# A two-layer decoder trunk on one core: expert products in two passes by branches, whole-unit weight splits, and operands at even places

## The chip, the core and the metric

One NeuronCore of a Trainium2 chip runs the whole program. The metric is device time in microseconds (us), the median of several executions; lower is better. The engines named below are TensorE (PE; its weight loads are PEld), VectorE (DVE), ScalarE (ACT), GpSimd (POOL) and the queue engine that issues transfers (SP). A letter q behind an engine's name (PEq, DVEq) is its sequencer.

## The reference

256 tokens of width 1024 pass through two layers. Each layer has an attention mixer and a channel mixer; the channel mixer of layer 0 is a dense SwiGLU of width 3584, and that of layer 1 sends each token to its best two of eight experts. All of it is float32.

```python
def moe_swiglu(h, router_w, w_gate, w_up, w_down):
    t = h.reshape(B * S, D)                                  # 256 x 1024
    logits = (t @ router_w).astype(jnp.float32)
    top_v, top_i = lax.top_k(logits, TOP_K)                  # 2 of 8
    top_w = jax.nn.softmax(top_v, axis=-1)
    gates = jnp.sum(jax.nn.one_hot(top_i, N_EXPERTS) * top_w[..., None], axis=1)
    y = jnp.zeros_like(t)
    for e in range(N_EXPERTS):                               # each 3 x 1024 x 3584 weights
        y = y + gates[:, e:e + 1] * ((jax.nn.silu(t @ w_gate[e]) * (t @ w_up[e])) @ w_down[e])
    return y
```

With the inputs that the reference draws by default, the eight experts get 68, 62, 71, 84, 60, 28, 77 and 62 tokens (counted by running the reference's own routing). Experts 1, 4, 5 and 7 have at most 64.

## The kernel before

**Precision.** Every weight is split in two float32r parts: ACT copies a piece into the high part (L139, the tile w), DVE subtracts that from the original to get the low part (L159, the tile lo). Activations are split likewise. A product is three matmuls into one PSUM bank: high by high, high by low, low by high.

**The stream of weights.** The class Stream brings the weights in units of 128 partitions x 2048 columns (1 MB) into a ring of raw buffers (L120, issued by SP when the buffer's last reader, usually DVE's subtraction, is done), and splits them in pieces of 1024 columns, in a fixed order that a planner has written out. There are four places for high parts and four for low ones; in layer 1 the attention mixer's accumulator row becomes a fifth high place (widen), and the mixer's q, k and v buffers and one more become raw buffers (extend), so that the expert stage has 12 raw buffers. get() hands the next piece to PE; pump() and rest() issue the splits for pieces to come as far as the places allow.

**The expert stage** (experts, 8 experts x 7 chunks of 512 columns). For each pair of experts, pick() builds one-hot matrices from the token's place in its expert (posm), gather() multiplies them with the tokens' high and low parts (L972), and ACT copies the up to 128 tokens of an expert, as columns, into xe (L974). A chunk then runs in this order: gate (wide, L986, 24 matmuls of 128 x 512), SiLU on ACT (L1107), up (wide, L986, 24 matmuls), and down of the chunk before (L1029, 24 matmuls into ps_y). Within the next gate's matmuls, turn() transposes the activation (L1012, four transposes) and splits it (L400 on ACT, L401 on DVE). The product of SiLU and up (L1125) is made by DVE in two halves among the down matmuls. After the last chunk of an expert, finish() puts the gated rows back in place with matmuls by the transposed one-hots (back, L1055, L1056), among the matmuls of the next expert. In the very last chunk down comes after its own transposes.

**The overflow.** An expert with more than 128 tokens is completed in a branch (overflow, L1159) that all engines read and skip here: each loads the largest count into a register (L1158) and branches over a loop that has hundreds of matmuls.

**Places.** A tile's place is worked out from the order and the sizes of the tiles in the pools. Before, the raw buffers begin at byte 28,640 of a partition, which is 895 x 32, an odd multiple of 32 bytes, and so do the splits, xe and the activation's parts (g_hi, g_lo); the dense layer's and the mixers' activations (dg_hi, onT_hi, hT_hi) lie at even multiples.

## Time and profile before

| what | value |
|---|---|
| median of 3 runs | 1525.04 us (1522.99 to 1525.07) |
| the profiled execution | 1523.73 us, of which 1521.6 us are its span |
| mean granted TensorE clock | 0.995 of full speed |
| busy share of the span | PE 98%, DVE 85%, ACT 69%, POOL 1% |
| moved by transfers | 481.81 MB, mean 317 GB/s |

The span runs from the first to the last instruction; 2.1 us of the execution lie outside it. A busy PE is not a PE at its peak, since matmuls are pipelined and their shown durations overlap: the time from the start of one matmul to the start of the next is what counts.

### The profile page before, as it was taken

What the parts mean: (1) busy time and instruction counts of PE and PEld (TensorE: products, weight loads), DVE (VectorE), ACT (ScalarE), POOL (GpSimd) and SP (SyncE); (2) the same over time, 40 slices, a digit from 0 to 9 for tenths busy, and PEclk for the clock granted to TensorE, in tenths of its full rate; (3) what the DMA queues carried; (4) which work ended last, traced back from release to release, by engine and by line L of the source; (5) the groups of instructions that cost most, each with busy time, mean ns of one, the idle gap of its engine ahead of it and who ended that gap; (6) DMA issues with size and microseconds to landing.
All of it is one profiled execution on the core that took longest, in us unless ns stands there. A gap on an engine that the chain in (4) does not pass through costs nothing.

```text
span 1521.6 us, 21909 instructions
## 1 busy us (share of the span) xinstructions
PE 1492.3 (98%) x7985; PEld 1271.4 (84%) x7985; DVE 1288.5 (85%) x1601; ACT 1054.0 (69%) x1404; POOL 20.2 (1%) x20
## 2 busy tenths in 40 slices
PE   8999999999999899999999999999999999999998
PEld 7988999999898688888888888888888888888886
DVE  5988877777876678899889889889889888988987
ACT  5575644444666578777787777777777778777775
POOL 1000000000020000000000000000000000000000
PEclk9999999999999999999999999999999999999999
DMA  9974778778572379999989999989999998999980
GB/s 368 415 271 166 295 269 324 292 278 314 192 264 111 123 294 368 380 368 360 367 332 353 376 375 358 370 331 350 374 377 363 362 364 334 358 374 372 352 344 28
DMA packets 68481, 481.81 MB, mean 317 GB/s; under 512 B 7953, under 2 KB 8593, under 8 KB 10770
## 3 DMA queue, kind: packets, MB, share of 16 engines
q1 hardware_dynamic: 68178, 480.33, 83.0%
q8 instruction: 63, 1.03, 0.3%
q14 instruction: 48, 0.39, 0.1%
q0 software_dynamic: 192, 0.05, 0.0%
HBM read 479.25 MB, written 1.05 MB: 316 GB/s over the span
## 4 chain that ended last, share of the span: by engine, by line
PE 63%; DVE 1%; issue 0%; ACT 0%; DVEq 0%
PE ps_y L1029 20%; PE ps_gate L986 20%; PE ps_up L986 20%; PE ps_gt L1012 2%; PE ps_g L972 1%; PE ps_sc L1055 0%; PE ps_sc L1056 0%; DVE lo L159 0%; DVE pick L877 0%; PE ps_sc L1079 0%; ACT g_hi L400 0%; PE ps_b L882 0%; DVE fin L1087 0%; ACT junk L355 0%; DVE x_sb L1081 0%
## 5 line engine op out<-in xcount | busy, mean ns | idle before, releaser
L159 DVE TENSOR_TENSOR lo<-raw,w 128x1024 fp32r<-128x1024 f32 x810 | 949.3, 1219 | 43.5 <-ACT w L139 39.8
L139 ACT ACTIVATE w<-raw 128x1024 fp32r<-128x1024 f32 x810 | 832.1, 1059 | 187.6 <-PE ps_gu L350 73.6
L986 PE MATMUL ps_gate<-w,xe 128*128 128x512 f32 x896 | 302.9, 398 | 0.0
L986 PE MATMUL ps_up<-w,xe 128*128 128x512 f32 x896 | 289.8, 392 | 0.0
L986 PEld LDWEIGHTS ps_up<-w,xe 128*128 128x128 f32 x896 | 168.3, 188 | 36.2
L986 PEld LDWEIGHTS ps_gate<-w,xe 128*128 128x128 f32 x896 | 168.4, 188 | 34.3
L986 PE MATMUL ps_up<-lo,xe 128*128 128x512 f32 x448 | 175.4, 392 | 0.3
L986 PE MATMUL ps_gate<-lo,xe 128*128 128x512 f32 x448 | 175.1, 391 | 0.1
L1029 PE MATMUL ps_y<-w,g_hi 128*128 128x512 f32 x440 | 137.7, 392 | 0.0
L1029 PE MATMUL ps_y<-lo,g_hi 128*128 128x512 f32 x440 | 137.3, 391 | 0.0
L1029 PE MATMUL ps_y<-w,g_lo 128*128 128x512 f32 x440 | 137.2, 391 | 0.0
L349 PE MATMUL ps_gu<-dT_hi,w 128*128 128x256 f32 x432 | 121.2, 281 | 0.0
L350 PE MATMUL ps_gu<-dT_lo,w 128*128 128x256 f32 x432 | 120.8, 280 | 0.0
L351 PE MATMUL ps_gu<-dT_hi,lo 128*128 128x256 f32 x432 | 120.7, 279 | 0.0
L400 ACT ACTIVATE g_hi<-ps_gt 128x512 fp32r<-128x512 f32 x55 | 32.9, 598 | 105.4 <-PE ps_gt L1012 105.4
L401 DVE TENSOR_TENSOR g_lo<-ps_gt,g_hi 128x512 fp32r<-128x512 f32 x55 | 38.1, 692 | 78.6 <-ACT g_hi L400 77.8
L986 PEld LDWEIGHTS ps_up<-lo,xe 128*128 128x128 f32 x448 | 84.2, 188 | 19.8 <-DVE lo L159 2.0
L986 PEld LDWEIGHTS ps_gate<-lo,xe 128*128 128x128 f32 x448 | 84.4, 188 | 16.5 <-DVE lo L159 0.8
L1029 PEld LDWEIGHTS ps_y<-lo,g_hi 128*128 128x128 f32 x440 | 82.7, 188 | 17.9
L1029 PEld LDWEIGHTS ps_y<-w,g_lo 128*128 128x128 f32 x440 | 82.7, 188 | 17.6
L1029 PEld LDWEIGHTS ps_y<-w,g_hi 128*128 128x128 f32 x440 | 82.4, 188 | 17.3
L349 PEld LDWEIGHTS ps_gu<-dT_hi,w 128*128 128x128 f32 x432 | 81.3, 188 | 1.4 <-issue 0.2
(295 smaller groups left out, 1935.9 us busy)
## 6 DMA issues: line engine op xcount, KB each, us to landing
raw<-in_w_moe_dram SPq DMA_DIRECT2D x336, 1024.0 KB, 6.6
raw<-in_w_early_dram SPq DMA_DIRECT2D x114, 1024.0 KB, 7.0
raw<-in_w_early_dram SPq DMA_DIRECT2D x6, 512.0 KB, 9.3
gate<-in_ada_b_dram SPq DMA_DIRECT2D x4, 512.0 KB, 5.6
x_sb<-in_x_dram SPq DMA_DIRECT2D x1, 1024.0 KB, 7.5
out_dram<-fin SPq DMA_DIRECT2D x4, 256.0 KB, 2.1
fg<-in_final_g_dram SPq DMA_DIRECT2D x1, 512.0 KB, 3.3
cn<-in_consts_dram SPq DMA_DIRECT2D x1, 192.0 KB, 13.4
```

Of the source, the lines that this page charges most:

```text
L139: self.nc.scalar.activation(hi, raw, AF.Copy)
L159: self.nc.vector.tensor_sub(parts[1], raw, parts[0].bitcast(F32))
L349: nc.tensor.matmul(out_, lh, rh, start=start, stop=False)
L350: nc.tensor.matmul(out_, lh, rl, start=False, stop=False)
L351: nc.tensor.matmul(out_, ll, rh, start=False, stop=stop)
L400: nc.scalar.activation(hi, src, AF.Copy)
L401: nc.vector.tensor_sub(lo, src, hi.bitcast(F32))
L972: nc.tensor.matmul(ps[:, i], part[:, b, k * P:(k + 1) * P], pk[:, b], start=(b == 0), stop=(b == NB - 1))
L986: nc.tensor.matmul(ps, lh, w[:, c], start=(k == 0 and lh is xe_hi and w is hi), stop=(k == KD - 1 and lh is xe_lo))
L1012: nc.tensor.transpose(ps[:, i], act[:, (f0 + i) * P:(f0 + i + 1) * P], ident)
L1029: nc.tensor.matmul(y_ps[e][hf], lh, w[:, hf * 512:(hf + 1) * 512], start=(ch == 0 and f == 0 and lh is g_hi and w is hi), stop=(last and l ...
```

## The change

1. **Two passes.** If an expert has at most 64 tokens (NARROW), its tokens are gathered to every second column (slotm = posm x 2). The columns 0, 2, 4, ... of the 256 that hold its high and its low part side by side are then one stationary operand: 64 high columns and 64 low ones. Two matmuls, by the high and by the low part of the weight, give all four products, the low rows in partitions 64 to 127. folded() adds these to the upper rows: ACT copies them to SBUF, one matmul of 64 rows (onto) adds them in PSUM. In turn() the narrow transposes write each row to two columns (eight transposes in place of four). In down the rows are left apart; the transposed one-hot of the pair (now made by POOL, pickb) adds both when the rows are put back.
2. **Branches.** The counts of all experts are loaded into PE registers, and every group of products (twelve or eight matmuls), the transposes and the folds stand in a branch on the expert's count, on PE alone: by_width() twelve times a chunk for products, once for the transposes; add() twice.
3. **Whole units.** In the expert stage a unit is split by one instruction of 2048 columns on each of ACT and DVE. There are two such high and low places in the split tiles, and the mixer's q and k buffers are two more high ones, v one more low one; they are no raw buffers any more, and the further raw buffer is gone: 8 raw buffers remain.
4. **Places.** The tiles are reordered and gaps are put between pools, so that raw buffers, splits, xe and the activations' parts all begin at multiples of 512 bytes.
5. The product of SiLU and up is one DVE instruction of 512 columns, behind the fold; SiLU moves behind the gate's fold, into the up matmuls.

```diff
+    def whole(self, high, low):
+        self.size = RAW
+        ...
     def prep(self, lazy=False):
-        u, o, what = self.pieces[self.next_prep]
+        u, o, n, what = self.pieces[self.next_prep]
         self.load()
-        raw = self.raw[u][:, o:o + SPLIT]
+        raw = self.raw[u][:, o:o + n]
...
+    def half(self):
+        if not self.rest_of:
+            hi, lo = self.get()
+            self.rest_of = [(hi[:, c:c + SPLIT], lo[:, c:c + SPLIT]) for c in range(0, hi.shape[-1], SPLIT)]
+        return self.rest_of.pop(0)
...
+    gap(keep, 384)
+    cn = keep.tile([P, C_MASK], F32, name="cn")
...
+    gap(keep, 160)
+    gap(tiny, 96)
...
+        if l:
+            whi = [qkv_pool.tile([P, RAW], F32R, tag=tag, name="whi2") for tag in "qk"]
+            ws.whole(whi, [qkv_pool.tile([P, RAW], F32R, tag="v", name="wlo2")])
...
+        nc.gpsimd.tensor_scalar(less, iota, NARROW - 0.5, -float(NARROW), ALU.is_gt, ALU.mult)
+        nc.gpsimd.tensor_sub(base, iota, less)
+        nc.gpsimd.tensor_scalar(onto[:, NARROW:], ident[:, NARROW:], 0.0, None, ALU.mult)
+        nc.gpsimd.tensor_copy(onto[:, :NARROW], ident[:, NARROW:])
...
+        def by_width(e, wide, narrow):
+            with tc.If(held[e] > NARROW) as cmp:
+                wide()
+            with cmp.Else():
+                narrow()
...
             for j in range(2):
+                slot = outer.tile([P, CAP], F32, name="slot", bufs=2)
+                nc.gpsimd.tensor_scalar(slot, less, stretch[:, e + j:e + j + 1], None, ALU.mult)
+                nc.gpsimd.tensor_add(slot, slot, base)
+                pb = outer.tile([P, NB, CAP], F32, name="pickb", bufs=2)
+                for b in range(NB):
+                    nc.gpsimd.tensor_scalar(pb[:, b], slot, posm[:, b, e + j:e + j + 1], None, ALU.is_equal)
+                rows_of.append(pb)
...
+            nc.vector.tensor_scalar(stretch, ps_p[:, 2], NARROW + 0.5, 1.0, ALU.is_lt, ALU.add)
+            nc.vector.tensor_tensor(slotm, posm, stretch[:, None, :].to_broadcast([P, NB, E]), ALU.mult)
...
+            nc.vector.tensor_copy(count, ps_p[:, 2])
+            held.extend(nc.tensor.value_load(count[0:1, e:e + 1], min_val=0, max_val=S) for e in range(E))
             overflow(l, hT, posm, gating, gates, most, [put.args[-1] for put in puts])
...
             def wide(e, ps):
                 for k in range(KD):
-                    xe_hi, xe_lo = xe[e][k]
-                    c = halves[k % 2]
                     if k % 2 == 0:
-                        hi, lo = ws.get()
-                    for lh, w in ((xe_hi, hi), (xe_hi, lo), (xe_lo, hi)):
-                        nc.tensor.matmul(ps, lh, w[:, c], start=(k == 0 and lh is xe_hi and w is hi),
-                                         stop=(k == KD - 1 and lh is xe_lo))
+                        hi, lo = ws.half()
+                        def products(*passes):
+                            n = 0
+                            for kk in range(k, k + 2):
+                                both = xe[e][kk]
+                                for part, w in passes:
+                                    n += 1
+                                    nc.tensor.matmul(ps, both[:, part], w[:, halves[kk % 2]], start=(k == 0 and n == 1),
+                                                     stop=(k == KD - 2 and n == 2 * len(passes)))
+                        first, second, even = slice(0, CAP), slice(CAP, 2 * CAP), slice(0, 2 * CAP, 2)
+                        by_width(e, partial(products, (first, hi), (first, lo), (second, hi)),
+                                 partial(products, (even, hi), (even, lo)))
                     yield k
+            def folded(ps):
+                t = pool.tile([P, FC], F32R, name="fold", bufs=2)
+                nc.scalar.activation(t[NARROW:], ps[NARROW:], AF.Copy)
+                by = partial(nc.tensor.matmul, ps, onto[NARROW:], t[NARROW:], start=False, stop=True, ...)
+                def add(e):
+                    with tc.If(held[e] <= NARROW):
+                        by()
+                return add
...
-                        nc.tensor.transpose(ps[:, i], act[:, (f0 + i) * P:(f0 + i + 1) * P], ident)
-                    split(hi[:, :n], lo[:, :n], ps)
+                    by_width(e, partial(turns, slice(0, P), slice(0, P)),
+                             partial(turns, slice(0, NARROW), slice(0, P, 2), slice(1, P, 2)))
+                    split(both[:, :n, 0], both[:, :n, 1], ps)
...
+                    add = folded(pg)
                     act = pool.tile([P, FC], F32, name="act")
-                    nc.scalar.activation(act, pg, AF.Silu)
...
                     for k in wide(e, pu):
+                        if k == 3:
+                            add(e)
+                            nc.scalar.activation(act, pg, AF.Silu)
```

## Rows read from the trace of the kernel before

**Rows 1.** The profile page, its part 1 (busy time, share of the span, instructions of each engine) and, of its part 2 (the span in 40 equal slices), the busy tenths of the DMA engines and the GB/s.

```profile
PE 1492.3 (98%) x7985; PEld 1271.4 (84%) x7985; DVE 1288.5 (85%) x1601; ACT 1054.0 (69%) x1404; POOL 20.2 (1%) x20
...
DMA  9974778778572379999989999989999998999980
GB/s 368 415 271 166 295 269 324 292 278 314 192 264 111 123 294 368 380 368 360 367 332 353 376 375 358 370 331 350 374 377 363 362 364 334 358 374 372 352 344 28
```

**Rows 2.** The view of stretches, one row for each (from:to in us, its length, then busy us and instructions of PE, PEld, DVE, ACT and POOL, the granted clock, the mean busy share of the DMA engines, GB/s): the start with layer 0's mixer, the dense layer, layer 1's mixer with the routing, the expert stage.

```profile
0.00:160.00 160.00, 147.84 (x996) 132.01 (x997) 127.32 (x247) 97.84 (x219) 10.25 (x14) 0.99 0.76 300
160.00:392.00 232.00, 232.00 (x1645) 215.56 (x1644) 179.35 (x225) 107.85 (x142) 0.00 (x0) 1.00 0.80 295
392.00:534.00 142.00, 132.94 (x903) 118.64 (x901) 99.17 (x207) 88.00 (x200) 9.92 (x6) 0.98 0.48 171
534.00:1492.00 958.00, 957.38 (x4360) 789.32 (x4360) 860.66 (x897) 744.06 (x819) 0.00 (x0) 1.00 0.93 355
```

**Rows 3.** The chain of work that ended last, in order of time (start us, us, what), over one chunk of an expert, into the next.

```profile
702.20 4.10 PE ps_gate L986 x18
706.29 0.44 PE ps_gt L1012 x4
706.73 1.38 PE ps_gate L986 x6
708.11 5.48 PE ps_up L986 x24
713.59 5.49 PE ps_y L1029 x24
719.08 4.12 PE ps_gate L986 x18
```

**Rows 4.** The same view of stretches as in Rows 2: one of the start, in which many loads are under way at once, and the steady part of the expert stage.

```profile
10.00:70.00 60.00, 57.23 (x455) 55.95 (x455) 47.53 (x76) 33.70 (x62) 1.68 (x3) 0.97 1.02 418
540.00:1480.00 940.00, 939.55 (x4272) 774.58 (x4271) 849.09 (x887) 731.81 (x804) 0.00 (x0) 1.00 0.94 360
600.00:640.00 40.00, 40.00 (x183) 32.95 (x182) 34.22 (x36) 30.06 (x34) 0.00 (x0) 1.00 0.97 372
```

**Rows 5.** DVE and ACT in order of time (start us, us from the first start to the last end, engine, line, what, how many; in brackets the idle time before).

```profile
708.01 8.03 DVE L159 TENSOR_TENSOR lo<-raw,w 128x1024 fp32r<-128x1024 f32 x7
...
708.68 6.00 ACT L139 ACTIVATE w<-raw 128x1024 fp32r<-128x1024 f32 x6
```

**Rows 6.** Groups of instructions by line and shape (line, engine, operation, out<-in, shapes, count | busy us, mean ns of one | idle us before, and what ended it): the DVE and ACT work of the expert stage.

```profile
L159 DVE TENSOR_TENSOR lo<-raw,w 128x1024 fp32r<-128x1024 f32 x810 | 949.3, 1219 | 43.5 <-ACT w L139 39.8 <-PE ps_w L350 2.6 <-ACTq L1159 0.5
L139 ACT ACTIVATE w<-raw 128x1024 fp32r<-128x1024 f32 x810 | 832.1, 1059 | 187.6 <-PE ps_gu L350 73.6 <-PE ps_y L1029 41.7 <-PE ps_gate L986 17.0
...
L401 DVE TENSOR_TENSOR g_lo<-ps_gt,g_hi 128x512 fp32r<-128x512 f32 x55 | 38.1, 692 | 78.6 <-ACT g_hi L400 77.8
...
L400 ACT ACTIVATE g_hi<-ps_gt 128x512 fp32r<-128x512 f32 x55 | 32.9, 598 | 105.4 <-PE ps_gt L1012 105.4
...
L1058 DVE SCALAR_TENSOR_TENSOR x_sb<-ps_sc,gates,x_sb 128x512 f32<-128x512 f32 x28 | 20.9, 746 | 0.0
...
L1050 DVE TENSOR_TENSOR y_lo<-yt,y_hi 128x512 fp32r<-128x512 f32 x14 | 9.6, 685 | 0.0
...
L1042 DVE TENSOR_TENSOR yt<-ps_y,gate 128x512 f32<-128x512 f32 x14 | 9.6, 683 | 0.0
```

**Rows 7.** The same view: PE's matmuls of 512 columns, those of the expert stage (both operands at odd places) and those of the dense layer (stationary at an even place, moving at an odd one), the transposes, and a weight load.

```profile
L986 PE MATMUL ps_up<-lo,xe 128*128 128x512 f32 x448 | 175.4, 392 | 0.3
...
L1029 PE MATMUL ps_y<-lo,g_hi 128*128 128x512 f32 x440 | 137.3, 391 | 0.0
...
L986 PEld LDWEIGHTS ps_gate<-lo,xe 128*128 128x128 f32 x448 | 84.4, 188 | 16.5 <-DVE lo L159 0.8
...
L349 PE MATMUL ps_d<-w,dg_hi 128*128 128x512 f32 x112 | 44.4, 397 | 0.0
L350 PE MATMUL ps_d<-lo,dg_hi 128*128 128x512 f32 x112 | 44.4, 396 | 0.0
```

**Rows 8.** The overflow's branch, line L1159: the sequencers' instructions there (count: duration ns min/median/max, first and last start us).

```profile
L1159 ACTq COMPARE_BRANCH  x1: 50/50/50, 526.1 to 526.1; - x1
L1159 POOLq COMPARE_BRANCH  x1: 45/45/45, 526.1 to 526.1; - x1
L1159 PEldq COMPARE_BRANCH  x1: 3446/3446/3446, 526.2 to 526.2; - x1
...
L1159 DVEq COMPARE_BRANCH  x1: 72/72/72, 526.5 to 526.5; - x1
L1159 DVEq EVENT_SEMAPHORE  x1: 21/21/21, 527.1 to 527.1; - x1
...
L1159 PEldq EVENT_SEMAPHORE  x1: 51/51/51, 529.7 to 529.7; - x1
```

**Rows 9.** PE and its weight loads in order of time, where the first expert's gate begins behind a short idle time (columns as in Rows 5).

```profile
534.75 0.19 PEld L986 LDWEIGHTS ps_gate<-w,xe 128*128 128x128 f32 x1
534.78 0.48 PE L986 MATMUL ps_gate<-w,xe 128*128 128x512 f32 x1
...
535.10 0.40 PE L986 MATMUL ps_gate<-lo,xe 128*128 128x512 f32 x1
```

**Rows 10.** The load of the overflow's count into PE's register (columns as in Rows 8), and PE behind the branch (columns as in Rows 5).

```profile
L1158 PEldq TENSOR_LOAD <-most x1: 492/492/492, 525.6 to 525.6; - x1
...
529.93 0.77 PE L972 MATMUL ps_g<-pick,h_hi 128*128 128x256 f32 x2 [4.60 <-PEq L1159]
...
533.72 0.69 PE L882 MATMUL ps_b<-cn,pick 128*128 128x128 f32 x2
```

**Rows 11.** Groups of POOL's instructions (columns as in Rows 6).

```profile
L862 POOL CAST ident<-cn 128x128 bf16<-128x128 f32 x1 | 1.2, 1156 | 10.4 <-issue 10.4
...
L862 POOL CAST ones<-cn 128x128 bf16<-128x128 f32 x1 | 0.3, 288 | 0.0
```

More of the change, by code (lines that the diff above doesn't have):

```diff
@@ L43 @@
 CAP = P
+NARROW = 64
 V_ADAB, V_ATTN, V_FFN, V_QN, V_KVN, V_OUT, V_FB = 0, 48, 56, 64, 66, 67, 75
@@ L105, in extend, with widen @@
             self.load()
-    def widen(self, pool, tag):
-        self.turns.insert(0, (pool, tag, 1))
+    def widen(self, tile_):
+        self.turns.insert(0, Place(tile_))
+    def whole(self, high, low):
+        self.size = RAW
+        turns = []
+        for t, old, more in zip(self.split, (self.turns, self.low_turns), (high, low)):
+            new = [Place(x) for x in more]
+            for at in range(0, SPLIT_BUFS * SPLIT, RAW):
+                new.append(Place(t, at))
+                new[-1].last = max(x.last for x in old if x.tile is t and at <= x.at < at + RAW)
+            turns.append(new)
+        self.turns, self.low_turns = turns
     def load(self, most=None):
@@ L169, in pump @@
         while self.next_prep < len(self.pieces) and (most is None or n < most):
-            if self.pieces[self.next_prep][2] is None:
+            _, _, size, what = self.pieces[self.next_prep]
+            if what is None:
+                if size > self.size:
+                    break
                 ahead = len(self.turns) - (self.prepped >= self.given + need)
-                if self.prepped >= self.released + ahead:
+                if self.prepped >= self.released + ahead or self.turns[0].last >= self.released:
                     break
@@ L194, in get @@
     def get(self, n=1):
+        assert not self.rest_of
         self.settle()
@@ L341, in trunk_kernel @@
     for y in order:
-        pieces.append((*place[y], y[1:] if y[0] == "ada" else None))
+        u, o = place[y]
+        if y[0] not in "gud":
+            pieces.append((u, o, SPLIT, y[1:] if y[0] == "ada" else None))
+        elif not o:
+            pieces.append((u, o, sources[u][1], None))
     ws = Stream(nc, sources, pieces, raw_pool, split_pool, fold)
@@ L1021, in down, with products @@
                 for f in range(NFC):
-                    hi, lo = ws.get()
-                    g_hi, g_lo = g[f]
-                    last = ch == CH - 1 and f == NFC - 1
-                    steps = [(hf, lh, w) for lh, w in ((g_hi, hi), (g_hi, lo), (g_lo, hi)) for hf in range(2)]
-                    if last:
-                        steps.sort(key=lambda s: s[0])
-                    for hf, lh, w in steps:
-                        nc.tensor.matmul(y_ps[e][hf], lh, w[:, hf * 512:(hf + 1) * 512],
-                                         start=(ch == 0 and f == 0 and lh is g_hi and w is hi),
-                                         stop=(last and lh is g_lo))
+                    hi, lo = ws.half()
+                    both = g[f]
+                    def products(*passes):
+                        first, last = ch == 0 and f == 0, ch == CH - 1 and f == NFC - 1
+                        steps = [(n, hf) for n in range(len(passes)) for hf in range(2)]
+                        if last:
+                            steps.sort(key=lambda s: s[1])
+                        for n, hf in steps:
+                            part, w = passes[n]
+                            nc.tensor.matmul(y_ps[e][hf], both[:, part], w[:, halves[hf]], start=(first and n == 0),
+                                             stop=(last and n == len(passes) - 1))
+                    first, second, even = slice(0, CAP), slice(CAP, 2 * CAP), slice(0, 2 * CAP, 2)
+                    by_width(e, partial(products, (first, hi), (first, lo), (second, hi)),
+                             partial(products, (even, hi), (even, lo)))
                     yield f
@@ L1119, in experts @@
                             step()
-                    parts = deque(slice(c, c + FC // 2) for c in (0, FC // 2))
+                    parts = deque([slice(0, FC)])
+                    add = folded(pu)
                     def product():
                         if parts:
+                            add(e)
                             c = parts.popleft()
```

108 lines of the change are left out of this document (61 added, 47 removed).

## The prediction

> **What bounds the kernel now.** I read the page first. PE is busy for 98% of the span, but DVE is at 85% and the DMA engines are at nine tenths from the middle of the span on [rows 1], so the share alone does not say what a faster PE would give. The view of stretches divides it: the expert stage is 958 of 1521.6 us, with PE busy throughout, DVE for 90% and the DMA engines for 93% of it [rows 2]. The chain that ended last decides: over whole chunks it is PE alone, matmul behind matmul, without a wait for a split or a load [rows 3]. One chunk, from the first gate matmul to the next chunk's, lasts 719.08 - 702.20 = 16.88 us, and its parts are gate 4.10 + 1.38, transposes 0.44, up 5.48, down 5.49 [rows 3]. 24 matmuls in 5.48 us are 0.228 us each, start to start. So PE is the bound, and 56 chunks of 16.88 us are 945 us. The reader is to see the second thing too: DVE and the loads are close behind it, and they are what a chunk with less PE work runs into.
>
> **What the change removes from PE.** Four experts have at most 64 tokens, so 28 of 56 chunks are narrow. Each loses 24 of 72 matmuls and gains two folds and four transposes: 48 x 0.228 = 10.9, folds 0.46, transposes 2 x 0.44 = 0.88, in all 12.3 us. A stationary operand that takes every second column could load more slowly; the load takes 188 ns [rows 7] and a matmul 228, and even if each pair then took 0.30 us, PE would stand at 15.8 us, no worse than what follows.
>
> **What holds a narrow chunk then.** Three things, each from its own row.
>
> Loads. A chunk is six units of 1.049 MB. In the start, with many loads under way, the DMA engines gave 418 GB/s at a full share [rows 4]: 2.51 us a unit, 15.05 us a chunk. Over the expert stage they gave 360 GB/s at a share of 0.94 [rows 4]; if that was already their way of working there, full means 383 GB/s and 16.4 us. I lean to the first, since the second is measured with gaps between the loads, and keep both.
>
> DVE. Seven subtractions of 1024 columns take 8.03 us [rows 5], so one follows another by (8.03 - 1.22) / 6 = 1.135 us. From 692 ns at 512 columns to 1219 at 1024 [rows 6] a column costs 1.03 ns; 2048 columns take 1.135 + 1.054 = 2.19 us, six of them 13.1. The product and the low part of the activation are one 512-column instruction each, 0.69 less the same overlap of 0.08 us: 1.2 together. Putting back an expert's rows is 2 x 0.683 + 2 x 0.685 + 4 x 0.746 = 5.7 us [rows 6], with overlap 5.1, or 0.7 a chunk. Sum 15.1 us. With pieces of 1024 it would be 12 x 1.135 + 2.0 = 15.6, so whole units give DVE half a microsecond a chunk, worth nothing where PE is the bound.
>
> ACT. Six copies in 6.00 us [rows 5] follow each other by 0.99 us; the slope from 598 ns to 1059 is 0.90 ns a column [rows 6], so a unit takes 1.91 and six take 11.5 us. SiLU, the high part and the two new fold copies are 4 x 0.5 = 2.0. ACT also stands still before each high part, 105.4 us over 55 times, for the transposes [rows 6]: 1.9 us. That is 15.4 us, and the fold copies add two more places where ACT waits for PE, with four high places to have run ahead.
>
> Three floors of 15.05 to 15.4 us do not mesh perfectly: I take 15.8 us for a narrow chunk, a gain of 1.08 us, times 28 = **-30 us**. The ends: 15.05 us gives -51, 16.4 gives -13.
>
> **Wide chunks.** They keep 72 matmuls, and the other engines stay under 16.88 us, so they keep their time unless the places change the matmul. With both operands at odd places a matmul shows 391 to 392 ns, with the stationary one at an even and the moving one at an odd place 396 to 397 [rows 7]: a step of 5 ns when the two differ. The dense layer's down, the value projection and the output projections, 624 matmuls that differ now, would lose it: **-3 us**. No row shows two even operands of this kind at 512 columns often enough. If being even is worth the same step again, 72 x 28 x 0.005 = 10 us come off; if it costs it, 10 us come on; I take nothing. The Trainium skill (TensorE: Matmul & The Clock Gate, Back-to-back issue gap) gives N / 2.4 + 2.5 ns, 216 ns at 512 columns; the 228 ns here lie above it, and if the new places brought that figure, an estimate from the page, wide chunks would lose 24 us more and the sum would be 1470.
>
> **The start of the stage.** PE loads eight counts into registers ahead of the overflow's branch, where PE is the last to come out [rows 8, 10]. One load takes 0.49 us [rows 10]; together they cost between 0.49, if they overlap, and 3.9 us: I take **+3 us**, since the next step waits for all of them. POOL makes the first pair's pickb, eight instructions of 128 x 128, while PE is in the branch and the gather. POOL's casts of that shape take 0.29 and 1.16 us [rows 11]; PE's transposes come at 533.72 [rows 10], 8 us behind the counts, so 2.3 to 9.2 us of work cost 0 to 1.4 us, and I take 0. Later pairs' one-hots can be made many chunks ahead.
>
> **The branches.** There are 15 a chunk. A sequencer's compare and branch took 45 to 72 ns on ACT, POOL and DVE, and 3,446 ns on PE, which skipped the longest code [rows 8]. The arms here skip a few instructions, so I take the short price. It is hidden by the matmuls that are queued ahead: 12 matmuls last 2.7 us. I cost it at nothing; without that cover it would be 15 x 0.07 = 1 us a chunk.
>
> **Sum** against the profiled execution: 1523.7 - 30 - 3 + 3 = 1493.7, or **1494 us**; the median of the runs is 1.3 us above that execution, so the gain is 31 us or 2.0%. Its own range, from the ends of the narrow chunk and the places: 1470 to 1512.
>
> **Rival 1, slower: PE empties at branches.** Counts that other engines wait for must agree on both arms. The skipped overflow shows how the program settles this: a semaphore instruction on PE's sequencer (51 ns) behind the branch [rows 8]. If the shorter arm ends in such an instruction, and it waits for the matmuls before it, PE runs dry. The price: the rest of the last matmul 0.39 - 0.23 = 0.16, the instruction 0.05, the way from it to the next matmul 0.1 to 0.2 (529.7 to 529.93 with another wait between [rows 8, 10]), and a first matmul of 0.48 in place of 0.39 [rows 9]: about 0.45 us. The shorter arm is the narrow one for the twelve groups of products, the wide one for transposes and folds. A narrow chunk is then 12.3 + 12 x 0.45 = 17.7 us (+0.8), a wide one 16.88 + 1.35: 28 x 0.8 + 28 x 1.35 = +60 us, **1585 us**. It decides from a price of about 0.3 us, where a narrow chunk reaches 15.9 and the wide ones lose 25 us. For it: the instruction is there in the trace. Against it: it is seen once, on an idle PE, and a last matmul could carry the count itself. If both arms waited everywhere, 15 times 0.45, the time would pass 1750.
>
> **Rival 2, slower: a branch that has to fetch code.** PE's one branch took 3.45 us [rows 8]. If one branch in every chunk did, a narrow chunk would hide it (12.3 + 3.4 = 15.7) and a wide one not: 28 x 3.4 = 97 us, less the gain, **1590 us**. For it: twelve more groups of matmuls in each chunk are code that is skipped. Against it: the other engines' branches were short. The Trainium skill (Runtime: NRT & Kernel Launch, Instruction fetch mechanics) says that a taken branch to a target outside the fetched window stalls for a fetch; the 3.45 us agree with that, and short skips mostly stay inside it.
>
> **Rival 3: the loads are the bound already.** At 383 GB/s a narrow chunk takes 16.4 us and the gain is 13 us: **1511 us**. For it: a share of 0.97 at 372 GB/s in a full stretch [rows 4]. Against it: 418 GB/s in the start. Four fewer raw buffers would push the same way.
>
> **How the numbers follow.** The forecast has 0.44; a gain beyond its range, by the places, 0.08; rival 3 has 0.12, rival 1 0.25, rival 2 0.05, and 0.06 remain for a gain and a branch cost that cancel. What this kernel's runs can tell from no change is about 0.2%. Faster: 0.44 + 0.08 + 0.12 = 0.64; slower 0.30; same 0.06. The range must reach into rival 1, which alone has more than two in ten: 1465 to 1600 us leaves out some 0.05 below and 0.13 above.
>
> **What would show it.** Right: in narrow chunks PE has gaps that end in a split or a load, the chunk lasts 15.5 to 16.2 us, the DMA share is full and the rate above 400 GB/s; wide chunks stay at 16.9 us; 512-column matmuls show 385 to 392 ns everywhere. Rival 1: semaphore rows on PE's sequencer by the hundred, and in the chain "issue" or PEq pieces between groups of eight matmuls. Rival 2: a few dozen compare-and-branch rows of over 3 us. Rival 3: a full share at under 390 GB/s. The prediction is wrong if a branch costs PE more than 0.3 us, if ACT's waits at the folds hold up the splits, or if other counts of tokens arrive.

## The result, and the profile after

The changed kernel takes 1534.33 us (1533.29 to 1536.63, four runs) beside 1524.45 us for the kernel before on the same chip: a ratio of 1.0066, with a 95% interval of 1.0054 to 1.0079. It is slower by 0.7%, where 1494 us were forecast. The profiled execution has a span of 1531.5 us, 9.9 us above the 1521.6 before.

From the page after: PE's busy time, and by slices of 38 us the DMA engines' share in tenths and what they moved.

```profile
PE 1436.7 (94%) x7481; PEld 1159.0 (76%) x7481; DVE 1272.4 (83%) x1212; ACT 1073.7 (70%) x1180; POOL 51.4 (3%) x56
DMA  9974778778571249999999899998999998999992
GB/s 374 403 269 165 289 273 314 288 280 307 191 273 58 82 171 349 358 351 358 418 368 342 339 348 339 349 354 317 368 426 396 381 414 346 339 352 353 361 416 117
```

PE shows 504 matmuls fewer than before [rows 1], and the rate now goes up and down in the expert stage: its slices above 400 GB/s belong to narrow experts. The view of stretches (columns as in [rows 2]), for the whole stage and for two stretches of narrow chunks:

```profile
534.00:1496.00 962.00, 900.50 (x3870) 675.04 (x3871) 840.86 (x513) 761.44 (x601) 32.17 (x29) 0.99 0.92 356
720.00:760.00 40.00, 37.19 (x156) 25.78 (x155) 38.99 (x26) 34.91 (x26) 0.00 (x0) 1.00 1.00 418
1120.00:1160.00 40.00, 37.11 (x149) 25.83 (x150) 38.76 (x22) 36.53 (x28) 0.00 (x0) 1.00 1.01 419
```

And PE's time line where two chunks begin, first a wide one (expert 2) and its successor, then a narrow one (expert 4) and its successor; each row is the first gate matmul.

```profile
861.20 0.39 PE L1071 MATMUL ps_gate<-whi,xe 128*128 128x512 f32 x1
879.21 0.39 PE L1071 MATMUL ps_gate<-whi,xe 128*128 128x512 f32 x1
...
1111.91 0.39 PE L1071 MATMUL ps_gate<-whi,xe 128*128 128x512 f32 x1
1127.05 0.39 PE L1071 MATMUL ps_gate<-whi,xe 128*128 128x512 f32 x1
```

The narrow chunk takes 15.14 us. Six units at 418 GB/s take 15.05, and the DMA engines are at a full share; but DVE is busy for 97% of these stretches too. The view of waits over the expert stage (560 to 1500 us; who waited for whom, us in all, times, longest) decides between them:

```profile
PE ps_gate L1071 <- DVE wlo L183: 20.6, 30, 1.0
```

It has no line in which an engine waits for a load. By the order of loads and splits, each unit of the undisturbed narrow chunks landed at least 5 us before ACT began to split it. So a narrow chunk is bound by DVE's splits, and the loads just keep up.

The wide chunk takes 18.01 us, where it took 16.88 [rows 3]. With the first gate of every chunk read in this way, the whole difference can be laid out. (An expert's stretch runs from its first gate matmul to the next expert's, so it begins with the last down of the expert before.)

| stretch | before | after | difference |
|---|---|---|---|
| up to the first gate matmul | 534.8 | 549.5 | +14.7 |
| the four wide experts (0, 2, 3, 6) | 479.6 | 513.2 | +33.6 |
| the four narrow experts (1, 4, 5, 7) | 472.7 | 433.4 | -39.3 |
| from the last gate on | 34.5 | 35.5 | +1.0 |
| sum | 1521.6 | 1531.5 | +9.9 |

(The parts are rounded, the sums are the spans.) So the narrow experts gained more than forecast, and two terms that were put at 0 and +3 took it all back: the wide chunks and the way to the first gate.

**Wide chunks.** The views of the two lines of branches: instructions, nanoseconds (least, median, most), first and last start. L1088 is the fold's branch in add(), L933 that of by_width().

```profile
L1088 PEldq COMPARE_BRANCH  x168: 67/176/358, 556.1 to 1509.3; - x168
L1088 PEldq EVENT_SEMAPHORE  x56: 51/51/51, 559.9 to 1398.3; - x56
...
L933 PEldq COMPARE_BRANCH  x1093: 65/176/428, 549.3 to 1518.6; - x183
```

There are 56 semaphore instructions, two for each of 28 wide chunks, all at the fold, which has no arm for wide experts. The branches at L933, whose two arms both hold matmuls, have none. The time line around one of them:

```profile
869.38 0.39 PE L1071 MATMUL ps_up<-wlo,xe 128*128 128x512 f32 x1
869.61 0.39 PE L1071 MATMUL ps_up<-whi,xe 128*128 128x512 f32 x1
870.12 0.60 ACT L1231 ACTIVATE act<-ps_gate 128x512 f32<-128x512 f32 x1 [0.28 <-PEq L1088]
870.31 0.49 PE L1071 MATMUL ps_up<-whi,xe 128*128 128x512 f32 x1 [0.32 <-PEq L1088]
870.64 0.39 PE L1071 MATMUL ps_up<-wlo,xe 128*128 128x512 f32 x1
```

From 869.38 to 869.61 is the usual 0.23 us. The next matmul comes 0.70 us later, when the one before has ended and the sequencer has passed the semaphore, and the one after that 0.33 us later: 0.57 us lost, twice a chunk. Each of the 56 semaphore instructions starts 0.04 us behind the end of the last matmul ahead of it, so PE has run empty by then. The reader should see that PE was idle for the sequencer, and that ACT's SiLU waits for the same instruction: it stands for the fold's matmul in the count that SiLU waits for.

**The way to the first gate.** The eight loads of counts (their three instructions), the overflow's branch on PE, and PE's first matmuls behind it:

```profile
L1037 PEldq TENSOR_LOAD <-count x8: 299/302/494, 531.7 to 536.9; - x8
L1037 PEldq FUSED_REGOPS  x8: 146/146/160, 532.3 to 537.3; - x8
L1037 PEldq SEQ_ASSERT  x8: 18/18/24, 532.5 to 537.5; - x8
...
L1279 PEldq COMPARE_BRANCH  x1: 6187/6187/6187, 538.0 to 538.0; - x1
...
544.48 0.77 PE L1052 MATMUL ps_g<-pick,h_hi 128*128 128x256 f32 x2 [14.59 <-PEq L1279]
```

The loads stand one behind another from 531.72 to 537.58, 0.73 us each, and the branch that took 3.45 us [rows 8] takes 6.19. PE is idle for 14.59 us, where it was for 4.60 [rows 10]. The remaining 4.6 of the 14.7 us were lost earlier: the router's first matmul starts at 524.10 in place of 519.54. The rows of the router's matmuls, before and after:

```profile
L909 PE MATMUL ps_r<-rw,rT x32: 274/276/276, 519.5 to 523.0; 128*128 128x128 f32 x32
```

```profile
L987 PE MATMUL ps_r<-rw,rT x32: 274/276/276, 524.1 to 527.6; 128*128 128x128 f32 x32
```

### The profile page after: what moved, and what is told of

Same layout as the page of the kernel before. It is cut to its first block, busy times and chain, and to the rows that moved or that the text cites. A ratio compares the mean times of both kernels' runs of the same rounds, so it can differ in the third digit from the quotient of the medians.

```text
span 1531.5 us, 20974 instructions
## 1 busy us (share of the span) xinstructions
PE 1436.7 (94%) x7481; PEld 1159.0 (76%) x7481; DVE 1272.4 (83%) x1212; ACT 1073.7 (70%) x1180; POOL 51.4 (3%) x56
## 5 line engine op out<-in xcount | busy, mean ns | idle before, releaser
L183 DVE TENSOR_TENSOR wlo<-raw,whi 128x2048 fp32r<-128x2048 f32 (+1 forms) x474 | 927.3, 1976 | 71.4 <-ACT whi L162 64.0
L162 ACT ACTIVATE whi<-raw 128x2048 fp32r<-128x2048 f32 (+1 forms) x474 | 771.3, 1661 | 109.0 <-PE ps_gu L396 77.3
L1071 PE MATMUL ps_up<-whi,xe 128*128 128x512 f32 x672 | 242.3, 401 | 8.6 <-PEq L1088 8.6
L1071 PE MATMUL ps_gate<-whi,xe 128*128 128x512 f32 x672 | 243.0, 401 | 0.3 <-PEq L1088 0.3
L1141 PE MATMUL ps_y<-whi,g 128*128 128x512 f32 x664 | 204.4, 401 | 9.4 <-PEq L1088 9.4
L1071 PE MATMUL ps_gate<-wlo,xe 128*128 128x512 f32 x448 | 182.3, 407 | 22.1 <-DVE wlo L183 20.6
L1071 PE MATMUL ps_up<-wlo,xe 128*128 128x512 f32 x448 | 178.8, 399 | 7.6 <-DVE wlo L183 7.4
L1071 PEld LDWEIGHTS ps_up<-whi,xe 128*128 128x128 f32 x672 | 127.7, 190 | 48.9 <-ACT whi L162 17.5
L1071 PEld LDWEIGHTS ps_gate<-whi,xe 128*128 128x128 f32 x672 | 127.9, 190 | 24.5 <-issue 0.7
L1141 PE MATMUL ps_y<-wlo,g 128*128 128x512 f32 x440 | 141.3, 400 | 3.6 <-DVE wlo L183 2.4
L1071 PEld LDWEIGHTS ps_up<-wlo,xe 128*128 128x128 f32 x448 | 85.6, 191 | 31.2 <-DVE wlo L183 15.2
```

The source lines that it names most:

```text
L162: self.nc.scalar.activation(hi, raw, AF.Copy)
L183: self.nc.vector.tensor_sub(parts[1], raw, parts[0].bitcast(F32))
L1071: nc.tensor.matmul(ps, both[:, part], w[:, halves[kk % 2]], start=(k == 0 and n == 1), stop=(k == KD - 2 and n == 2 * len(passes)))
L1141: nc.tensor.matmul(y_ps[e][hf], both[:, part], w[:, halves[hf]], start=(first and n == 0), stop=(last and n == len(passes) - 1))
```

## The experiments

Each kernel below is timed beside the kernel before; a chunk is undisturbed where no expert begins or ends near it. The last three columns are read from the trace as above: the start of the first gate matmul, and the length of an undisturbed chunk in the middle of an expert.

| kernel | median us | first gate | wide chunk | narrow chunk |
|---|---|---|---|---|
| before | 1524.0 to 1524.5 | 534.8 | 16.88 | |
| changed | 1534.33 | 549.5 | 18.01 | 15.05 to 15.15 |
| e1 small product for the skipped fold | 1527.18 | 552.0 | 17.70 | 15.0 to 15.15 |
| e2 counts loaded one by one | 1526.42 | 541.3 | 18.01 | 15.05 to 15.15 |
| e3 places odd again | 1538.59 | 545.1 | 18.32 | 15.0 to 15.15 |
| e4 all wide, no branches on a count | 1526.49 | 540.5 | 16.80 | |
| e5 folds merged into other arms | 1515.04 | 550.0 | 17.20 | 15.05 to 15.15 |
| e6 = e5 + e2 | 1506.22 | 540.6 | 17.20 | 15.05 to 15.15 |
| e7 = e6 + dense activation at odd places | 1501.62 | 536.7 | 17.20 | 15.05 to 15.15 |
| e8 = e4 + skipped folds | 1580.18 | 541.5 | 17.70 | |
| e9 = e7, fold copies later on ACT | 1516.16 | 535.8 | 17.20 | 15.87 |
| e10 = e4 + fold copies on ACT | 1531.09 | 540.6 | 16.80 | |
| e11 = e7, product later on DVE | 1501.11 | 535.2 | 16.80 | 15.4 to 15.5 |
| e12 = e4 + the other 13 branches | 1536.63 | 550.4 | 16.80 | |

### Four kernels that take the change apart

The theory after the comparison: wide chunks lose at the skipped folds alone, the start loses by the loads of the counts, and the early 4.6 us by the places. In the cuts of code, "..." stands for lines left out.

```diff
 e1:
+                none = partial(nc.tensor.matmul, ps[:NARROW, 0:64], onto[NARROW:, NARROW:], t[NARROW:, 0:64],
+                               start=False, stop=True, skip_group_check=True)
...
-                    with tc.If(held[e] <= NARROW):
-                        by()
+                    by_width(e, none, by)
```

> The changed kernel, with one difference: where a wide expert skips the fold, it now issues one small product instead (64 x 64 zeros by 64 columns), so that both arms of the two folds of a chunk end in a matmul and none in a semaphore instruction. The results are the same. Theory (PE empties at the skipped folds): the two gaps of 0.48 us in a wide chunk go and a product of about 0.05 us each comes; a wide chunk falls from 18.0 to about 17.15 us, 28 of them are 24 us, and the time is about 1510 us (1507 to 1515). Rival (the gaps only show where PE would have waited anyway, for ACT's copy behind the fold, for whole units or for the fewer raw buffers): the wait moves to the next matmul, a wide chunk stays above 17.7 us, and the time is 1526 us or more.

e1 came out at 1527.18 us, in the rival's range, and a wide chunk took 17.70 us, at its edge. But the wait has not moved as the rival has it: the fold's semaphores are gone, and the small product in their place is not cheap.

```profile
869.34 0.39 PE L1071 MATMUL ps_up<-whi,xe 128*128 128x512 f32 x1
869.65 0.24 PE L934 MATMUL ps_gate<-fold,onto 64*64 64x64 f32 x1
869.83 0.50 PE L1071 MATMUL ps_up<-whi,xe 128*128 128x512 f32 x1
870.16 0.40 PE L1071 MATMUL ps_up<-wlo,xe 128*128 128x512 f32 x1
```

From 869.34 to 870.16 are 0.82 us, where two matmuls in a row take 0.45: the product of 64 columns cost 0.37 us, not 0.05. (The median over all 56 such places is the same.) That part of the expectation was wrong, and the run decides for neither theory.

```diff
 e2:
+        def hold(e):
+            held.append(nc.tensor.value_load(count[0:1, e:e + 1], min_val=0, max_val=S))
...
             nc.vector.tensor_reduce(most, ps_p[:, 2], axis=AX.X, op=ALU.max)
+            nc.vector.tensor_copy(count, ps_p[:, 2])
...
-            nc.vector.tensor_copy(count, ps_p[:, 2])
-            held.extend(nc.tensor.value_load(count[0:1, e:e + 1], min_val=0, max_val=S) for e in range(E))
...
             next(ahead)
             next(ahead)
+            hold(0)
             next(picked)
...
+                        if k == 4 and ch == 2 and e + 1 < E:
+                            hold(e + 1)
```

> The changed kernel, with the counts loaded one by one: only expert 0's count is loaded ahead of the first gate matmul, behind the first gather's matmuls; each further count is loaded in chunk 2 of the expert before, behind queued gate matmuls. The copy that makes the counts readable stands right behind the largest count. Theory (the eight loads stand one behind another on PE's sequencer, 0.68 to 0.84 us each): the first gate comes 6 to 7 us earlier than at 549.5, and the time is about 1528 us. Rival (the loads cover another wait, POOL's pickb or the overflow's branch): the first gate comes at 548 or later and the time stays at 1533 to 1535 us.

The first gate came at 541.3, 8.2 us earlier, and the time fell by 7.9 us. (The spans of the two profiled executions differ by 5.8 only: expert 0's first chunk takes 15.79 us in place of 14.01.) The branch starts 6.63 us behind the router's first matmul, as before the change, where the changed kernel needs 13.88. And more than the loads went: the overflow's branch was short again.

```profile
L1284 PEldq COMPARE_BRANCH  x1: 3407/3407/3407, 531.9 to 531.9; - x1
...
535.66 0.77 PE L1054 MATMUL ps_g<-pick,h_hi 128*128 128x256 f32 x2 [4.56 <-PEq L1284]
```

Over all traces of this study, the branch took 6.09 to 7.80 us in the five kernels that load eight counts ahead of it, and 3.33 to 3.87 us in the nine that don't. So it goes with the loads in all fourteen; why they lengthen it is open.

```diff
 e3:
-    gap(keep, 384)
+    gap(keep, 416)
...
-    gap(tiny, 96)
+    gap(tiny, 128)
...
-        gap(outer, 288)
+        gap(outer, 320)
```

> The changed kernel, with raw buffers, splits, xe, the activation's parts and the fold's rows moved back to odd multiples of 32 bytes, by 32 bytes more in three gaps; the activations of layer 0 and of the mixers stay at even multiples, as in the kernel before. Of the whole-unit places, those in the mixer's q, k and v buffers stay even. Theory (two even operands slow the early matmuls): the router's matmuls, 4.6 us late in the changed kernel, come back to where they are in the kernel before, and the first gate comes at about 545; in the expert stage, where a part of the operands now differ in kind, the wide chunks are 0 to 0.2 us longer, and the time is 1530 to 1535 us. Rival (the 4.6 us come from another part, such as the loads): the first gate stays at 549 to 550 us.

As the theory has it: the router's first matmul is back at 519.78, the first gate at 545.1. Not all of the 4.6 us is the places' doing, though. The dense layer, from its first gate matmul to its last of down, takes 239.86 us in the changed kernel and 237.05 before (e3: 237.04), so 2.8 lie there, and 0.8 in the two mixers, which e3 gives back as well. But 1.0 lies ahead of the first projection matmul (36.81 us from the start, before 35.81), and there kernels with even places vary from 34.8 to 36.9. The dense layer's rows show why, first of the changed kernel (both operands even), then of e3 (weights odd, activations even): the 256-column products by dT (the activation that goes into gate and up), and the 512-column products of down.

```profile
L395 PE MATMUL ps_gu<-dT_hi,whi x432: 277/284/682, 162.3 to 390.4; 128*128 128x256 f32 x144
L395 PE MATMUL ps_d<-whi,dg_hi x112: 389/392/500, 168.1 to 395.9; 128*128 128x512 f32 x112
```

```profile
L395 PE MATMUL ps_gu<-dT_hi,whi x432: 277/280/682, 161.3 to 386.6; 128*128 128x256 f32 x144
L395 PE MATMUL ps_d<-whi,dg_hi x112: 392/396/496, 166.9 to 392.1; 128*128 128x512 f32 x112
```

A 512-column matmul is 4 ns shorter with both operands at places of one kind, a 256-column one 4 ns longer, and the dense layer has 1344 of the short kind and 336 of the long. From start to start the means go from 116.8 to 119.9 ns and from 233.1 to 229.2: 1344 x 3.1 - 336 x 3.9 = 2.9 us, close to the 2.8 of the layer. In the expert stage, where nearly all are long, e3's partly mixed places cost 0.3 us a wide chunk, more than the 0.2 expected, and e3 as a whole is slower.

```diff
 e4:
-            with tc.If(held[e] > NARROW) as cmp:
-                wide()
-            with cmp.Else():
-                narrow()
+            wide()
...
-            nc.vector.tensor_scalar(stretch, ps_p[:, 2], NARROW + 0.5, 1.0, ALU.is_lt, ALU.add)
+            nc.vector.tensor_scalar(stretch, ps_p[:, 2], -0.5, 1.0, ALU.is_lt, ALU.add)
...
-            held.extend(nc.tensor.value_load(count[0:1, e:e + 1], min_val=0, max_val=S) for e in range(E))
...
+                return lambda e: None
```

> The changed kernel without two passes: every expert is wide, there are no branches on a count, no counts are loaded, no fold is copied or added, and the one-hots are not stretched. Places, whole units, buffers, the one-piece product and the later SiLU stay. Theory (the branches alone slow the wide chunks): a chunk takes 16.8 to 17.0 us as before, the first gate comes at 543 to 544 us, and the time is 1530 to 1540 us. Rival (whole units, four fewer raw buffers or the later SiLU slow a wide chunk too): a chunk takes 17.1 to 18.0 us and the time is 1548 to 1595 us.

16.80 us a chunk: whole units, eight raw buffers and the later SiLU cost a wide chunk nothing. It is 0.08 us shorter than before, which fits the places: in the kernel before the fifth high place (widen) lies at an even multiple of 32 bytes, unlike the other high places, so that some of its matmuls were of the mixed kind. No run takes this apart. The time, 1526.49 us, is below the expected 1530 to 1540, and the first gate, at 540.5, ahead of the expected 543. All of the 1.2 us between 16.80 and 18.01 come from the branches and what belongs to them.

### What a branch costs

```diff
 e5, in the narrow arm of the second group of up (and likewise of down):
+            def narrowed(products, *passes, by=None):
+                products(*passes)
+                if by is not None:
+                    by()
...
-                            add(e)
```

> The changed kernel, with the fold no longer a branch of its own: it stands at the end of the narrow arm of the products ahead of it (the second group of up, the second group of down), at the same place in PE's order. Only the second fold of a chunk that follows another expert's keeps its own branch: 8 of 112 folds and one in the last chunk. Theory (a skipped fold costs PE the 0.48 us in which it empties and 0.11 us in which the next matmuls start up, 0.59 in all, and the other branches cost nothing): a wide chunk takes 16.80 to 16.85 us, as in the kernel that is all wide, the first one of an expert 0.6 more; 28 wide chunks lose 31 us, and the time is about 1503 us (1499 to 1507, since the overflow's branch varies by some us). Rival (the twelve branches around products cost a share of the 1.2 us too): a wide chunk takes 17.2 us or more and the time is 1513 us or more.

e6 is e5 with e2's edit.

> The last kernel (merged folds) and the counts loaded one by one, both. Theory (two separate losses that add): the first gate comes at 541 to 542 us, wide chunks take 16.80 to 16.85 us, and the time is 1494 to 1498 us, faster than the kernel before by 27 to 30. Rival (the early start is given back later, as half of it seemed to be in the first chunk): 1500 us or more.

```diff
 e7, in dense(), ahead of dT_hi and behind dT_lo:
+        gap(pool, 32)
...
+        gap(pool, 480)
```

> Merged folds and late counts, and in the dense layer 0 the activation that goes into gate and up (dT_hi, dT_lo) is moved by 32 bytes to an odd multiple, while the weights' splits stay even. Theory (a 256-column matmul wants its two operands at places of different kind: 116 to 118 ns from start to start against 120): the 1344 gate and up matmuls of the dense layer give back about 3 ns each, the dense layer ends 4 us earlier, and the time is 4 us below the kernel without this move. Rival (the dense layer's time is set by the loads): no difference.

```diff
 e8, e4 with the fold copies, one count loaded, and this add():
+                def add(e):
+                    with tc.If(held[0] <= 0):
+                        by()
```

> The kernel that is all wide, with the two fold copies on ACT and the two fold branches of each chunk put back, on one count that is never zero, so that all 112 are skipped; there are no other branches on a count. It measures the disputed price by itself. Theory: 2 x 0.59 us a chunk, from 16.80 to 17.98 us, and the time is 1526.5 + 56 x 1.18 = about 1592 us (1588 to 1597). Rival (the price belongs to the branches around the products and their queue): a chunk stays under 17.4 us, and the time under 1560 us.

e8 gives the price of a skipped fold by itself: (17.70 - 16.80) / 2 = 0.45 us, 112 times, and 1580 us, less than the 1588 to 1597 expected but far above the rival's 1560. Every one has its semaphore. On PE's time line two steps across one take 875.97 - 875.13 = 0.84 us in place of 0.45:

```profile
L1085 PEldq COMPARE_BRANCH  x112: 201/201/339, 548.3 to 1551.7; - x112
L1085 PEldq EVENT_SEMAPHORE  x112: 51/51/51, 552.5 to 1554.7; - x112
...
875.13 1.00 PE L1068 MATMUL ps_up<-whi,xe 128*128 128x512 f32 x2
875.97 0.40 PE L1068 MATMUL ps_up<-wlo,xe 128*128 128x512 f32 x1
```

These 0.39 us compare with the 0.57 of the changed kernel, where by_width's compare and branch stands behind the semaphore: there 0.22 us pass from the semaphore's end to the next matmul, in e8 0.06 (medians). The other 0.06 us of the 0.45 were not traced. e5 gained 19 us and not 31, since a wide chunk stopped at 17.20, and so e6 missed its 1494 to 1498 too. But e6 and e7 show that the three losses add: 8.8 us by the counts, 4.6 by the dense layer's places, near what was expected. In e7 the dense layer takes 235.60 us for e6's 239.87, that is 4.3 of the 4.6, and its rows are as short as e3's:

```profile
L395 PE MATMUL ps_gu<-dT_hi,whi x432: 277/280/682, 161.5 to 385.5; 128*128 128x256 f32 x144
```

Still 0.40 us a wide chunk were unexplained, and e5's expectation had named the other branches as the rival, in whose range it had come out.

### What the last 0.4 us were

In e5 a wide chunk has one gap left, on PE's time line at its start:

```profile
870.87 0.39 PE L1071 MATMUL ps_gate<-whi,xe 128*128 128x512 f32 x1
871.37 0.50 PE L1071 MATMUL ps_gate<-wlo,xe 128*128 128x512 f32 x1
871.70 0.62 PE L1071 MATMUL ps_gate<-whi,xe 128*128 128x512 f32 x2
```

The first matmul by a low part starts 0.50 us behind its predecessor and the next one 0.33: 0.38 us more than two steps of 0.227, and it is a split that is late. My first theory was ACT, which in the changed kernels waits at the fold copy with the next high part behind it.

```diff
 e9, for the gate's copy (up's moves behind the first group of down):
-                    by = folded(pg)
...
                     for k in wide(e, pu, lambda: got[0]()):
+                        if k == 0:
+                            got.append(folded(pg))
```

> The kernel with merged folds, late counts and the moved activation of the dense layer (1501.6 us), with ACT's fold copies one place later in its order: the copy of the gate's rows stands behind the next unit's high part, the copy of up's rows likewise, while the folds themselves stay where they are on PE. Theory (the 0.40 us that a wide chunk still takes above the all-wide kernel's 16.80 come from ACT, which waits at the fold copy for PE to end the gate while the next high part stands behind it, so that DVE's low part comes late): a wide chunk falls from 17.20 to 16.80 to 16.95 us, narrow ones stay, and the time is 1490 to 1495 us. Rival (the rest is the price of the branches around the products): a wide chunk stays at 17.15 us or more and the time at 1500 us or more.

```diff
 e10, e4 with this in folded(), ahead of up and of down:
+                nc.scalar.activation(t[NARROW:], ps[NARROW:], AF.Copy)
```

> The kernel that is all wide and has no branches on a count (1526.5 us, 16.80 us a chunk), with nothing but the two fold copies on ACT put back ahead of up and of down; nobody reads them. Theory (the copies' place in ACT's order delays the splits): a chunk takes about 17.2 us and the time is about 1549 us (1543 to 1552). Rival (the copies fit into ACT's idle time, and the rest belongs to the branches): a chunk stays at 16.8 to 16.9 us and the time is 1526 to 1532 us.

That theory fell twice. With the copies later on ACT (e9) a wide chunk still took 17.20 us and a narrow one 15.87, since its folds now wait for the later copy, and with the copies alone (e10) a chunk took 16.80. DVE's own time line of e5 over a wide chunk shows what was late:

```profile
860.03 2.28 DVE L183 TENSOR_TENSOR wlo<-raw,whi 128x2048 fp32r<-128x2048 f32 x1
862.76 2.29 DVE L183 TENSOR_TENSOR wlo<-raw,whi 128x2048 fp32r<-128x2048 f32 x1 [0.45 <-ACT whi L162]
865.34 2.29 DVE L183 TENSOR_TENSOR wlo<-raw,whi 128x2048 fp32r<-128x2048 f32 x1 [0.29 <-ACT whi L162]
868.42 0.69 DVE L1252 TENSOR_TENSOR act<-act,ps_up 128x512 f32<-128x512 f32 x1 [0.79 <-PE ps_y L1147]
869.02 4.49 DVE L183 TENSOR_TENSOR wlo<-raw,whi 128x2048 fp32r<-128x2048 f32 x2
```

The product of SiLU and up has to wait for the group of down that now holds the fold, and DVE stands still for 0.79 us in front of it, with the next two low parts behind.

```diff
 e11:
-                        if f % 2:
+                        if f == 3:
                             product()
```

> The kernel with merged folds, late counts and the moved activation of the dense layer (1501.6 us), with the product of SiLU and up issued behind the fourth group of down in place of the second, so that DVE makes one more low part before it; the fold stays where it is on PE. Theory (the product stands in DVE's order and waits for the group of down that now holds the fold, 0.8 us in each chunk, and the next low parts come late, at the chunk's first matmuls by a low part): a wide chunk falls from 17.20 to 16.80 to 16.95 us, narrow ones stay, and the time is 1489 to 1496 us. Rival (the branches around the products): a wide chunk stays at 17.15 us or more and the time at 1500 us or more.

```profile
850.33 2.29 DVE L183 TENSOR_TENSOR wlo<-raw,whi 128x2048 fp32r<-128x2048 f32 x1 [0.29 <-ACT whi L162]
853.18 2.29 DVE L183 TENSOR_TENSOR wlo<-raw,whi 128x2048 fp32r<-128x2048 f32 x1 [0.56 <-ACT whi L162]
855.39 0.68 DVE L1259 TENSOR_TENSOR act<-act,ps_up 128x512 f32<-128x512 f32 x1
```

Now the product waits for nothing, and a wide chunk takes 16.80 us, to the hundredth that of e4. The theory was right for the wide chunk and wrong for the time, which is the same as e7's (1501.11 and 1501.62, not 1489 to 1496): the four wide experts gain 7.3 us (494.1 to 486.8), but the narrow ones give back 6.1 (435.0 to 441.1). The waits of DVE over three narrow chunks, of e7 (1085 to 1130 us) and then of e11 (1082 to 1128), show where:

```profile
DVE wlo L183 <- ACT whi L162: 0.6, 3, 0.2
```

```profile
DVE wlo L183 <- ACT whi L162: 1.6, 7, 0.3
```

DVE, which bounds a narrow chunk, now stands still 0.33 us a chunk longer for high parts, and the chunk is 0.35 longer.

```diff
 e12, e4 with by_width() back, without folds:
+            with tc.If(held[e] > 0) as cmp:
+                wide()
+            with cmp.Else():
+                narrow()
```

> The kernel that is all wide, with the thirteen branches of each chunk (twelve around products, one around transposes) put back on conditions that are always true, and with the eight loads of the counts; no folds, no fold copies. It measures the price of the branches by themselves. Theory (branches whose two arms both end in a matmul are hidden behind queued matmuls): a chunk takes 16.80 to 16.85 us and the time is 1532 to 1538 us, all of it above 1526.5 ahead of the first gate. Rival (they cost a wide chunk 0.4 us): 17.2 us a chunk and 1550 to 1560 us.

```profile
L933 PEldq COMPARE_BRANCH  x1458: 73/126/384, 550.1 to 1521.5; - x183
```

Thirteen branches a chunk, 26 compare-and-branch instructions, and 16.80 us: they cost a wide chunk nothing. All of e12's 10 us above e4 lie ahead of the first gate (550.4 against 540.5), with the eight loads and a branch of 6.35 us.

Together: e7 and e11 are 1.5% faster than the kernel before (0.9848, interval 0.9832 to 0.9865, and 0.9851, 0.9834 to 0.9867). The two passes are worth more than was forecast; what surrounded them cost what the forecast did not have.

## Why the prediction was wrong

- **What bounds the kernel** was read rightly: a wide chunk is PE's, matmul behind matmul, and e4 and e12 show it once more. A narrow chunk ran into DVE, with the loads at the 418 GB/s of the start close behind.
- **Narrow chunks**, put at -30 us, gave -39. Of 27 chunks 13, those in the middle of an expert, take 15.0 to 15.2 us, where 15.8 were allowed. DVE, whose floor was put at 15.1, is busy for 14.7 us of them. They lie under the 15.4 put down for ACT, so that sum was too high. Rival 3, loads at 383 GB/s, is out.
- **The branches** are the step that failed: "I cost it at nothing", hidden by queued matmuls. This holds for thirteen of fifteen (e12), but a skipped fold has no matmul in its arm that could carry the count, so a semaphore stands there and waits until PE is empty (0.04 us behind the last matmul's end, at all 56 places). Rival 1 had the mechanism and nearly the price, 0.45 us; e8 measured that by the chunk, and the changed kernel shows 0.57. It had the wrong places: it charged the shorter arm of all fifteen branches, and its own objection, that a last matmul could carry the count, is right wherever there is one. Two in a wide chunk and none in a narrow one, 56 x 0.57 = 31.9 us, make nearly all of the +33.6. The question that would have given it was which arms are empty, and the diff shows that: add() has no Else.
- **The start**, put at +3 us within 0.49 to 3.9, cost 10.1. Each load is three instructions on the sequencer, 0.73 us and not 0.49, and nothing overlaps: 5.9. The branch behind them grew by 2.7, which no term held, and the counts' copy on DVE comes some 1.5 us later than the largest count's did.
- **The places**, put at -3 us in the early layers, cost 3.6; the other 1.0 of the 4.6 lies ahead of the first projection and varies between kernels. The step counted the 624 early matmuls of 512 columns alone, by 5 ns [rows 7]; the 336 of down did gain 4 ns each, but the dense layer has 1344 of 256 columns, and there the sign is the other. The wide chunks, put at no change with 10 us to either side, gained 0.08 us each in e4. The Trainium skill (TensorE: Matmul & The Clock Gate, Back-to-back issue gap) gives the 216 ns at 512 columns for a single matmul, and about 131 ns for a stream of weight loads and matmuls; no row here shows either: from start to start the medians are 226 to 233 ns, and no step is under 223.
- **Rival 2**, a code fetch in each chunk, did not occur: the longest branch of by_width took 0.43 us.
- Sum by measured terms: 1521.6 - 39.3 + 33.6 + 4.6 + 10.1 + 1.0 = 1531.6, against a span of 1531.5; the terms are the stretches of the table, so they have to add up. By its time the outcome is slower, which had 0.30. By its mechanism it is the case that had 0.06, a gain and a cost that nearly cancel, where the start and the places are a part of the cost.

## What to carry to other kernels

Where a branch skips work that other engines count on, look for the arm that holds nothing: put the optional instruction at the end of an arm that has others, and the price goes. Load branch counts one at a time behind queued matmuls, not all ahead of the first use. And when a wait is moved, ask which in-order queue now has it at its head: here a product on DVE, not the copy on ACT that looked as guilty. Where two floors lie side by side, as DVE's and the loads' in a narrow chunk, a full share does not say which one holds; the waits do.

## What the runs showed of the hardware that was not expected

- A compare and branch over the same code took 3.3 to 3.9 us on PE's sequencer, and 6.1 to 7.8 us with eight register loads ahead of it. The Trainium skill (Runtime: NRT & Kernel Launch, Instruction fetch mechanics) puts a far branch's stall down to the fetch of code; no run here shows why the loads should lengthen it.
- The place of an operand counts in both directions: 512 columns take 392 ns with two operands at even multiples of 32 bytes and 396 with one even and one odd, 256 columns 284 and 280. Moving two tiles by 32 bytes took 4.3 us off the dense layer (e7).
- A matmul of 64 columns by a 64 x 64 operand, between matmuls of 512 columns, cost 0.37 us, more than a whole one of 512 columns (0.23); why is open (e1).
